# Two-bank PSUM tiles for the scores and the transposed probabilities of a windowed attention

## The chip, the cores and the metric

The kernel runs on one core of one Trainium2 chip. The metric is the device time of one execution in microseconds (us), taken as the median of several runs. The engines in this text are PE (TensorE, its weight loads are listed as PEld), DVE (VectorE), ACT (ScalarE), POOL (GpSimd) and SP, which issues DMAs. PSUM, the memory that PE writes its results to, is used here in eight banks, each of 512 float32 values on 128 partitions.

## The reference, cut to what matters

One decoder layer with two branches is computed for a prompt of 2048 positions and for a small group of 64 sampled positions. The change touches only the first branch, a grouped-query attention with a window of 128 positions, 8 query heads, 2 key/value heads and 64 values per head:

```python
d = qpos - kpos
band = (d >= 0) & (d <= WINDOW)                       # 128 queries against 256 keys
s = jnp.einsum('...qhgd,...khd->...hgqk', q, k).astype(jnp.float32) * (ATT_HEAD_DIM ** -0.5)
s = jnp.where(mask, s, NEG)
p = jax.nn.softmax(jnp.concatenate([s, sink], axis=-1), axis=-1)[..., :-1]
return jnp.einsum('...hgqk,...khd->...qhgd', p.astype(v.dtype), v)
```

The second branch (a gated linear attention) and the output projection follow it in the program and are the same before and after.

## The kernel before

`phase_a1` takes the first 400 us of the program, then `phase_gla` and `phase_out` follow. It works on 16 tiles of 128 prompt positions and one tile of 64 sampled ones. Each tile passes through the stages that `pipeline` (L537) staggers: `load`, `front` (norm of the input, with a broadcast of the row factors through a PSUM tile `pt` at L224), `dense` (the projection to q, k, v, 48 matmuls `pd` at L302 per tile), `rope`, `a` (`attna`, the scores and the softmax) and `b` (`attnb`, the product with the values). The first three tiles in `k.order1` are `early`: their `front` and `dense` are written ahead of the pipeline. The order of the instructions on each engine is made by the framework's scheduler from the program order, the priorities in `pipeline` and the buffers that are free. So a change of buffers moves instructions.

In `attna` the queries and keys are transposed on PE into `pq` (L387) and `pk` (L391). The scores of a tile come in two groups `g` of four heads. For each of two `j`, three products (L410: high times high, high times low, low times high) are written for `u` = 0 and `u` = 1 in turn. `u` is the key/value head: the product contracts over 64 rows, and `u` = 0 uses the lower 64 rows of the PE array, `u` = 1 the upper 64. Each `u` has its own PSUM tile `sc`. DVE then reads each head's 128x256 scores with the mask added (L415), which also gives the row maximum.

In `attnb` the probabilities are transposed on PE (L432) in blocks `pp` of four heads, two blocks per block of 128 keys. DVE copies the block of heads 0 to 3 (L433), which belong to `kv` = 0, and ACT that of heads 4 to 7, which belong to `kv` = 1. The value product `po` (L437) has one matmul for each `kv`, and they use the left 64 and the right 64 columns of the PE array.

The eight PSUM banks before are: two for `pd` (L302), three for `sc`, `pq` and `pk` in turn (pool `ps_s`), one for `po`, and two for `pp`, the broadcast `pt` and small uses at the start and in `gate` (pool `ps_t`). The projections of the second and third tile borrow banks of `ps_s` and `ps_o` (L294).

Of the kernel before, what the change touches and what calls it, by code (L numbers as in the profile page):

```python
# [95 lines left out]
def c_rows(k, sp, pp, w, name):  # L96

    nc = k.nc
    n = int(np.prod(w[0].shape[1:]))
    ps = pp.tile([P, 512], F32, tag="pt", name=name)  # L100
    for d in range(NC):
        r = slice(d % 4 * 32, d % 4 * 32 + 32)
        nc.tensor.matmul(ps[r, :n], k.cT[:, d, :], w[d], start=(d < 4), stop=(d >= 4),
                         tile_position=(0, r.start), skip_group_check=True)
    m = sp.tile([P, 512], F32, tag="crows", name="s" + name, bufs=2)
    nc.vector.tensor_copy(m[:, :n], ps[:, :n])
    return m


def modulation(k, cp, sp, pp, after):  # L110
# [14 lines left out]
    for j in range(NC + 1):  # L125
        if j < NC:
            m[j] = c_rows(k, sp, pp, [w[j][:, d] for d in range(NC)], f"mod{j}")
        if j > 0:
            d = j - 1
            ps = pp.tile([P, 2, 9], F32, tag="pt", name=f"modT{d}")  # L130
# [18 lines left out]
def phase_a1(k, cp, dp):  # L149
# [5 lines left out]
    with ExitStack() as es:  # L155
# [27 lines left out]
        with tc.tile_pool(name="a1m", bufs=1) as mp:  # L183
            for d, w in modulation(k, cp, mp, ps_t, lambda j: [load(early[n]) for n, m in ((0, 0), (1, 0), (2, 1)) if m == j]):
                nc.scalar.copy(whi[:, d, :], w)
                nc.vector.tensor_tensor(wlo[:, d, :], w, f(whi[:, d, :]), op=ALU.subtract)
# [16 lines left out]
        def front(i):  # L203
# [13 lines left out]
            else:  # L217
# [5 lines left out]
                pt = ps_t.tile([P, 1, 512], F32, tag="pt", name=f"pt{i}")  # L223
                nc.tensor.matmul(pt[:, 0, :T], k.ones[:T], diag[:T, :T], start=True, stop=True)  # L224
                nc.vector.tensor_tensor(h[:, :, :T], h[:, :, :T], pt[:, :, :T].to_broadcast((P, NC, T)), op=ALU.mult)
# [60 lines left out]
        def dense(i):  # L286
# [7 lines left out]
            banks = [(ps_s, "sc"), (ps_s if n == 1 else ps_o, "sc" if n == 1 else "po")] if n in (1, 2) else [(ps_d, "pd")] * 2  # L294
            pd = [pool.tile([P, 512], F32, tag=tag, name=f"pd{i}_{lo}") for (pool, tag), (lo, _) in zip(banks, rg)]
# [85 lines left out]
        def attna(i):  # L381
# [3 lines left out]
            pq = ps_s.tile([P, 4, P], F32, tag="sc", name=f"pq{i}")  # L385
# [4 lines left out]
            pk = ps_s.tile([P, 4, P], F32, tag="sc", name=f"pk{i}")  # L390
# [13 lines left out]
            for g in range(2):  # L404
                scs = [ps_s.tile([P, 2, 2 * P], F32, tag="sc", name=f"sc{i}_{g}_{u}") for u in range(2)]
                for j in range(2):
                    for n, (qa, ka) in enumerate(((0, kThi), (0, kTlo), (1, kThi))):
                        for u in range(2):
                            b = u * 64
                            nc.tensor.matmul(scs[u][:, j, :w], qT[b:b + 64, qa, 2 * g + j, :],  # L410
                                             ka[b:b + 64, sl, :], start=(n == 0), stop=(n == 2))
                for u in range(2):
                    for j in range(2):
                        h = 4 * u + 2 * g + j
                        nc.vector.tensor_tensor_reduce(  # L415
                            out=sm[:, h, :w], in0=scs[u][:, j, :w], in1=mk.rearrange("p a b -> p (a b)"), scale=1.0,
# [4 lines left out]
        def attnb(i):  # L421
# [23 lines left out]
        def attn_sample():  # L445
# [7 lines left out]
            pq = ps_t.tile([P, 4, P], F32, tag="pt", name="spq")  # L453
# [16 lines left out]
            for g in range(2):  # L470
                pt = ps_t.tile([P, 4, P], F32, tag="pt", name=f"spk{g}")
# [3 lines left out]
            pt = ps_t.tile([P, 4, P], F32, tag="pt", name="spkn")  # L475
# [4 lines left out]
            for bg in range(2):  # L480
                for kv in range(2):
                    sc = ps_s.tile([P, 2, 2 * P], F32, tag="sc", name=f"ssc{bg}_{kv}")
# [13 lines left out]
            pt = ps_t.tile([P, 4, P], F32, tag="pt", name="spp0")  # L496
# [3 lines left out]
            pt = ps_t.tile([P, 4, P], F32, tag="pt", name="spp1")  # L500
# [29 lines left out]
        def gate(i):  # L530
            if i == k.order1[8]:
                gate_rows(k, sp, ps_t, dp)
# [523 lines left out]
def gate_rows(k, sp, pp, dp):  # L1056
# [5 lines left out]
    for n in range(2):  # L1062
# [8 lines left out]
        for c0, c1 in ((0, P), (P, 192)):  # L1071
            pg = pp.tile([P, 512], F32, tag="pt", name=f"gb{n}_{c0}")
# [151 lines left out]
```

## Time and profile before

| | us |
|---|---|
| median of 3 runs | 1648.79 |
| lowest and highest run | 1646.57 and 1651.33 |
| the profiled execution | 1654.62 |
| its span in the trace | 1652.8 |
| mean granted clock of PE, of 1 | 0.962 |
| PE busy in the span | 1558.2 (94%) |

The span is the time from the first to the last instruction that the trace holds. The profiled execution is 1.8 us longer than its span, and 5.8 us (0.35%) longer than the median of the runs. The granted clock is the share of full speed that PE's throttle gave: 1.00 is 2.4 GHz, 0.5 is 1.2 GHz, and a value between them is a mean over a stretch with both levels. `phase_a1` ends at about 396 us of the span. From 414 to 1240 us the gated linear attention runs, and from 1322 us the output projection.

### The profile page before, as it was taken

How to read it: one execution, taken by the hardware profiler on the slowest of the kernel's cores; microseconds unless marked ns; L12 is line 12 of the kernel's file. 1: busy time of each engine (PE TensorE's matmuls, PEld its weight loads, DVE VectorE, ACT ScalarE, POOL GpSimd, SP SyncE). 2: the span in 40 equal slices, each digit the busy share in tenths (PEclk: the TensorE clock that was granted, in tenths of full speed). 3: DMA queues.
4: the chain of work that ended last, by engine and by line, in shares of the span. 5: the costliest groups of instructions: out<-in, count | busy, mean ns of one | idle time of the engine just before them, and what ended most of it. 6: DMA issues, size and time to landing. Idle time of an engine off the chain costs nothing.

```text
span 1652.8 us, 27244 instructions
## 1 busy us (share of the span) xinstructions
PE 1558.2 (94%) x9528; PEld 1357.5 (82%) x9528; DVE 1089.5 (66%) x2232; ACT 710.8 (43%) x1665; POOL 476.2 (29%) x553
## 2 busy tenths in 40 slices
PE   7789999897999999999999999999996699999998
PEld 5676766564999999899999999988895588888996
DVE  5886868855676788555777767778771165646442
ACT  3677857644334344333444445454451132313120
POOL 1885784733535444210212121124110000000000
PEclk9989999977999999999999999999998799999999
DMA  9875482672665554988676689876878977867632
GB/s 372 261 221 157 141 265 70 183 309 82 222 198 195 177 179 163 331 289 267 199 215 206 186 287 347 263 239 190 280 238 323 369 261 237 277 221 208 215 118 83
DMA packets 313182, 373.80 MB, mean 226 GB/s; under 512 B 37890, under 2 KB 229267, under 8 KB 307669
## 3 DMA queue, kind: packets, MB, share of 16 engines
q1 hardware_dynamic: 313044, 372.07, 68.9%
q8 instruction: 75, 1.23, 0.3%
q14 instruction: 63, 0.51, 0.1%
HBM read 248.91 MB, written 123.08 MB: 225 GB/s over the span
## 4 chain that ended last, share of the span: by engine, by line
PE 74%; DMA 9%; DVE 8%; ACT 3%; POOL 2%; issue 2%; SPq 2%; DVEq 0%; ACTq 0%; POOLq 0%
PE e L1045 10%; PE a L928 10%; PE d L928 10%; PE c L928 9%; PE q L583 9%; PE pd L302 6%; PE b L928 5%; PE g_l L784 3%; PE po L437 2%; PE sc L410 2%; PE pp L432 2%; DMA wo<-sw_e 1%; DMA s<-zm 1%; DMA o<-wo 1%; DVE tot L702 1%
## 5 line engine op out<-in xcount | busy, mean ns | idle before, releaser
L609 DVE TENSOR_TENSOR w<-r,w 128x512 fp32r<-128x512 f32 x272 | 203.5, 757 | 98.1 <-ACT w L608 88.0
L608 ACT CAST w<-r 128x512 fp32r<-128x512 f32 x272 | 165.8, 620 | 156.5 <-PE d L928 40.5
L928 PE MATMUL d<-x,w 128*128 128x384 f32 (+1 forms) x1152 | 206.7, 326 | 5.8 <-DVE u L937 2.3
L928 PE MATMUL c<-x,w 128*128 128x384 f32 (+1 forms) x1152 | 207.8, 326 | 3.4 <-ACT u L935 2.5
L928 PE MATMUL a<-x,w 128*128 128x384 f32 (+1 forms) x1152 | 209.4, 328 | 0.7 <-ACT w L608 0.7
L583 PE MATMUL q<-d_o,u_b 128*128 128x512 f32 (+1 forms) x960 | 189.7, 358 | 12.9 <-DMA d_o<-o 9.5
L928 PEld LDWEIGHTS d<-x,w 128*128 128x128 f32 x1152 | 189.0, 190 | 8.6 <-DVE u L937 2.8
L583 PEld LDWEIGHTS q<-d_o,u_b 128*128 128x128 f32 x960 | 162.3, 192 | 39.0 <-issue 13.0
L1045 PE MATMUL e<-wo,d_m 128*128 128x512 f32 x768 | 179.2, 394 | 13.9 <-DMA wo<-sw_e 13.9
L928 PEld LDWEIGHTS c<-x,w 128*128 128x128 f32 x1152 | 186.9, 189 | 5.7 <-ACT u L935 2.7
L928 PEld LDWEIGHTS a<-x,w 128*128 128x128 f32 x1152 | 188.4, 191 | 3.3 <-ACT w L608 1.0
L1045 PEld LDWEIGHTS e<-wo,d_m 128*128 128x128 f32 x768 | 146.0, 191 | 45.1 <-issue 14.7
L302 PE MATMUL pd<-whi,hs 128*128 128x512 f32 (+1 forms) x512 | 143.5, 362 | 7.1 <-DVE hs L240 4.4
L938 POOL TENSOR_TENSOR oc<-u,u 128x384 f32<-128x384 f32 (+1 forms) x48 | 69.4, 1445 | 273.5 <-DVE u L937 131.7
L302 PEld LDWEIGHTS pd<-whi,hs 128*128 128x128 f32 x512 | 92.4, 196 | 26.5 <-DVE hs L240 4.6
L928 PE MATMUL b<-x,w 128*128 128x384 f32 (+1 forms) x576 | 110.4, 332 | 0.5 <-ACT w L608 0.5
L928 PEld LDWEIGHTS b<-x,w 128*128 128x128 f32 x576 | 96.9, 193 | 2.1 <-ACT w L608 1.0
L302 PE MATMUL pd<-wlo,hs 128*128 128x512 f32 (+1 forms) x256 | 91.8, 361 | 0.0
L1011 ACT ACTIVATE s<-s 128x512 f32<-128x512 f32 (+1 forms) x64 | 41.1, 645 | 108.5 <-DMA s<-zm 106.6
L373 ACT ACTIVATE sm<-sm,nm,rs 128x256 f32<-128x256 f32 (+1 forms) x128 | 74.5, 587 | 7.8 <-DVE nm L369 7.4
L1023 DVE TENSOR_TENSOR s<-q,s 128x512 f32<-128x512 f32 (+1 forms) x40 | 23.1, 596 | 78.5 <-PE q L583 42.9
L736 DVE TENSOR_TENSOR KQ<-KQ,M 128x512 f32<-128x512 f32 (+2 forms) x115 | 71.9, 626 | 0.0
(249 smaller groups left out, 2638.7 us busy)
## 6 DMA issues: line engine op xcount, KB each, us to landing
r<-in_w_x SPq DMA_DIRECT2D x160, 256.0 KB
r<-tw SPq DMA_DIRECT2D x128, 256.0 KB
u_b<-sw_b SPq DMA_DIRECT2D x16, 2048.0 KB
x<-xd SPq DMA_DIRECT2D x14, 1536.0 KB
zm<-oc SPq DMA_DIRECT2D x48, 384.0 KB
xd<-sx SPq DMA_DIRECT2D x32, 512.0 KB
tw<-t SPq DMA_DIRECT2D x64, 256.0 KB
s<-zm SPq DMA_DIRECT2D x64, 256.0 KB
```

Source lines behind the costliest of these rows:

```text
L302: nc.tensor.matmul(pd[u][:T, :hi - lo], hs[:, d // 4, a, d % 4, :T], (whi, wlo)[b][:, d, lo:hi], start=(d == 0 and n == 0), stop=(d == NC ...
L373: nc.scalar.activation(sm[:, h, :w], sm[:, h, :w], AF.Exp, scale=0.125 if rq is None else rs[:, h:h + 1], bias=nm[:, h:h + 1], accum_out=d ...
L410: nc.tensor.matmul(scs[u][:, j, :w], qT[b:b + 64, qa, 2 * g + j, :], ka[b:b + 64, sl, :], start=(n == 0), stop=(n == 2))
L583: nc.tensor.matmul(ps[u][:, :s1 - s0], w[a][:, r, cs:cs + P], x[xr[n0]][:, b, s0:s1], start=(n0 == 0 and n == 0), stop=(n0 == len(rows) - ...
L608: nc.scalar.copy(w[:, 0], src)
L609: nc.vector.tensor_tensor(w[:, 1], src, f(w[:, 0]), op=ALU.subtract)
L736: nc.vector.tensor_tensor(out.rearrange("p a (n m) -> p a n m", m=m), x.rearrange("p a (n m) -> p a n m", m=m), M[r, b, at[n]:at[n + 1]].u ...
L784: nc.tensor.matmul(pl[:T, r, j, l - l0, :H], KQ[rr, l, j] if l else c["kT"][rr, j, :T], KQ[rr, l, 2 + j].rearrange("p (n s m) -> p n s m", ...
L928: nc.tensor.matmul(bank[b], wt[:, x, d], X[p][:, y, d], start=(p > 3 or p == 0) and d == 0 and n == 0, stop=(d == 3 and n == 2), skip_grou ...
L938: nc.gpsimd.tensor_tensor(oc[1][:, 1], t[2], t[1], op=ALU.add)
L1011: nc.scalar.activation(t[:, :N], t[:, :N], AF.Sigmoid)
L1045: nc.tensor.matmul(ps, mp[:, a, r, o0:o0 + T], wo[:, b, r, cs], start=(r == 0 and n == 0), stop=(r == 7 and n == 2))
```

## The change

The pools `ps_s` and `ps_t` are cut up in another way, with the same eight banks in all.

- `ps_s` now holds one tile of two banks. `scs[:, u]` is the bank of one `u`, so one tile holds a whole group of scores, for both `u`.
- `ps_t` now holds one tile `pq` of one bank (`one`) and one tile `pp` of two banks (`two`). `pq` serves the broadcast `pt`, the transposed queries `pq` and keys `pk` (which were in `ps_s`) and small uses. `pp` serves the transposed probabilities of all eight heads of a block of keys.
- The copies of `pp` are divided otherwise: DVE takes the first two heads of each bank (heads 0, 1, 4, 5) and ACT the last two of each (2, 3, 6, 7). Before, each took one bank.
- The projection of the second tile uses the two banks of `sc`, that of the third tile the bank of `pq` and the one of `po`.

No arithmetic is added or taken away.

```diff
-        ps_s = es.enter_context(tc.tile_pool(name="a1ps", bufs=3, space=PSUM))
+        ps_s = es.enter_context(tc.tile_pool(name="a1ps", bufs=1, space=PSUM))
...
-        ps_t = es.enter_context(tc.tile_pool(name="a1pt", bufs=2, space=PSUM))
+        ps_t = es.enter_context(tc.tile_pool(name="a1pt", bufs=1, space=PSUM))
+        one = lambda name: ps_t.tile([P, 512], F32, tag="pq", name=name)
+
+        two = lambda name: ps_t.tile([P, 2, 512], F32, tag="pp", name=name)
+        heads = lambda ap: ap.rearrange("p (h t) -> p h t", h=4)
...
-                pt = ps_t.tile([P, 1, 512], F32, tag="pt", name=f"pt{i}")
-                nc.tensor.matmul(pt[:, 0, :T], k.ones[:T], diag[:T, :T], start=True, stop=True)
+                pt = one(f"pt{i}")[:, :T]
+                nc.tensor.matmul(pt, k.ones[:T], diag[:T, :T], start=True, stop=True)
...
-            banks = [(ps_s, "sc"), (ps_s if n == 1 else ps_o, "sc" if n == 1 else "po")] if n in (1, 2) else [(ps_d, "pd")] * 2
-            pd = [pool.tile([P, 512], F32, tag=tag, name=f"pd{i}_{lo}") for (pool, tag), (lo, _) in zip(banks, rg)]
+            if n == 1:
+                pd = ps_s.tile([P, 2, 512], F32, tag="sc", name=f"pd{i}")
+                pd = [pd[:, u] for u in range(2)]
+            elif n == 2:
+                pd = [one(f"pd{i}_0"), ps_o.tile([P, 512], F32, tag="po", name=f"pd{i}_512")]
+            else:
+                pd = [ps_d.tile([P, 512], F32, tag="pd", name=f"pd{i}_{lo}") for lo, _ in rg]
...
-            pq = ps_s.tile([P, 4, P], F32, tag="sc", name=f"pq{i}")
+            pq = heads(one(f"pq{i}"))
...
-            pk = ps_s.tile([P, 4, P], F32, tag="sc", name=f"pk{i}")
+            pk = heads(one(f"pk{i}"))
...
-                scs = [ps_s.tile([P, 2, 2 * P], F32, tag="sc", name=f"sc{i}_{g}_{u}") for u in range(2)]
+                scs = ps_s.tile([P, 2, 2, 2 * P], F32, tag="sc", name=f"sc{i}_{g}")
...
-                for g in range(2):
-                    pt = ps_t.tile([P, 4, P], F32, tag="pt", name=f"pp{i}_{n}_{g}")
-                    for j in range(4):
-                        nc.tensor.transpose(pt[:, j, :], sm[:, g * 4 + j, n * P:(n + 1) * P], k.ident)
-                    (nc.scalar.copy if g else nc.vector.tensor_copy)(pT[:, n, g * 4:g * 4 + 4, :], pt)
+                pt = two(f"pp{i}_{n}").rearrange("p g (j t) -> p g j t", j=4)
+                for h in range(8):
+                    nc.tensor.transpose(pt[:, h // 4, h % 4, :], sm[:, h, n * P:(n + 1) * P], k.ident)
+
+                for u in range(2):
+                    (nc.scalar.copy if u else nc.vector.tensor_copy)(
+                        pT[:, n].rearrange("p (g j) t -> p g j t", g=2)[:, :, 2 * u:2 * u + 2], pt[:, :, 2 * u:2 * u + 2])
```

The rows below are instructions in the order in which one engine runs them: the line of the code, the operation, output and inputs by their names in the program (the first number in a name is the tile), the size of what moves, and the semaphores it waits on by engine. On PE, the second group of scores of tile 6 before (`sc6_1_0` is `u` = 0, `sc6_1_1` is `u` = 1, whose last five matmuls follow):

```order
L410 MATMUL sc6_1_0_2167<-kThi_338,qT6_2140 128x256
L410 MATMUL sc6_1_0_2167<-kTlo_339,qT6_2140 128x256
L410 MATMUL sc6_1_0_2167<-kThi_338,qT6_2140 128x256 x2
L410 MATMUL sc6_1_0_2167<-kTlo_339,qT6_2140 128x256
L432 MATMUL pp4_1_0_2062<-ident_137,sm4_1684 128x128 [waits DVE_49]
L432 MATMUL pp4_1_0_2062<-ident_137,sm4_1684 128x128 x3
L410 MATMUL sc6_1_0_2167<-kThi_338,qT6_2140 128x256
L302 MATMUL pd8_0_1996<-wlo_104,hs8_1663 128x512
L302 MATMUL pd8_0_1996<-whi_103,hs8_1663 128x512 x2
L302 MATMUL pd8_0_1996<-wlo_104,hs8_1663 128x512
L302 MATMUL pd8_0_1996<-whi_103,hs8_1663 128x512
L410 MATMUL sc6_1_1_2168<-kThi_338,qT6_2140 128x256 [waits DVE_49]
```

The same group on PE after, all twelve matmuls, behind the projection of tile 10:

```order
L311 MATMUL pd10_512_2432<-whi_103,hs10_2104 128x272 x2
L311 MATMUL pd10_512_2432<-wlo_104,hs10_2104 128x272
L311 MATMUL pd10_512_2432<-whi_103,hs10_2104 128x272
L419 MATMUL sc6_1_2144<-kThi_338,qT6_2118 128x256 [waits DVE_49]
L419 MATMUL sc6_1_2144<-kThi_338,qT6_2118 128x256
L419 MATMUL sc6_1_2144<-kTlo_339,qT6_2118 128x256 x2
L419 MATMUL sc6_1_2144<-kThi_338,qT6_2118 128x256 x4
L419 MATMUL sc6_1_2144<-kTlo_339,qT6_2118 128x256 x2
L419 MATMUL sc6_1_2144<-kThi_338,qT6_2118 128x256 x2
```

The six matmuls of `u` = 0 ran one after another before, ahead of the six of `u` = 1; now the two alternate. On PE, the four value matmuls of tile 4 before (`v3` and `v4` are the values of its two key blocks, with one matmul per `kv` each):

```order
L437 MATMUL po4_2048<-pT4_2049,v3_1164 64x512 [waits Activation_49]
L432 MATMUL pp4_1_1_2068<-ident_137,sm4_1684 128x128 [waits DVE_49]
L432 MATMUL pp4_1_1_2068<-ident_137,sm4_1684 128x128 x3
...
L437 MATMUL po4_2048<-pT4_2049,v3_1164 64x512 [waits Activation_49]
L437 MATMUL po4_2048<-pT4_2049,v4_1382 64x512
...
L437 MATMUL po4_2048<-pT4_2049,v4_1382 64x512 [waits Activation_49]
```

On PE, the transposes and the value product of tile 5 after:

```order
L440 MATMUL pp5_1_2255<-ident_137,sm5_1911 128x128 [waits Activation_49]
L440 MATMUL pp5_1_2255<-ident_137,sm5_1911 128x128 x7
L448 MATMUL po5_2242<-pT5_2243,v4_1372 64x512 x2
L396 MATMUL pq7_2354<-ident_137,rq_7_2082 128x128 [waits DVE_49]
L396 MATMUL pq7_2354<-ident_137,rq_7_2082 128x128 x3
L311 MATMUL pd11_0_2700<-whi_103,hs11_2318 128x512 [waits DVE_49]
L311 MATMUL pd11_0_2700<-wlo_104,hs11_2318 128x512
L311 MATMUL pd11_512_2701<-whi_103,hs11_2318 128x272 [waits Activation_49]
L311 MATMUL pd11_512_2701<-wlo_104,hs11_2318 128x272
L448 MATMUL po5_2242<-pT5_2243,v5_1613 64x512 [waits Activation_49]
L448 MATMUL po5_2242<-pT5_2243,v5_1613 64x512
```

Before, three separate places held the four matmuls of a tile; now two places hold two each. On ACT, the copies of tile 6's probabilities before, with the rows around the second:

```order
L433 COPY pT6_2512<-pp6_0_1_2519 128x512 [waits PE_49,Activation_49]
...
L331 COPY lr_60<-raw10_2458 128x16
L433 COPY pT6_2512<-pp6_1_1_2531 128x512 [waits PE_49]
L278 CAST sx6_11_2364<-s6_11_2362 128x512 [waits DMAHW6_49,DVE_49]
L278 CAST sx2_11_2370<-s2_11_2368 128x512 [waits DMAHW7_49,DVE_49]
```

And on ACT after:

```order
L443 COPY pT6_2484<-pp6_0_2485 128x2x256 [waits DVE_49]
L232 ACTIVATE h12_2349<-h12_2349,B_70,A_69 128x128 [waits DVE_49]
L232 ACTIVATE h12_2349<-h12_2349,B_70,A_69 128x128 x7
L443 COPY pT6_2484<-pp6_1_2496 128x2x256 [waits DVE_49]
L382 ACTIVATE sm7_2366,dn7_2404<-sm7_2366,nm7_2402,rs87_2406 128x256 [waits DVE_49,Pool_49]
```

ACT's copy waited for PE's transposes before; now it waits for DVE, whose own copy of the same two banks goes first.

## Rows read from the trace of the kernel before

**Rows 1.** The page: span and busiest engines, with share of the span.

```profile
span 1652.8 us, 27244 instructions
PE 1558.2 (94%) x9528; PEld 1357.5 (82%) x9528; DVE 1089.5 (66%) x2232; ACT 710.8 (43%) x1665; POOL 476.2 (29%) x553
```

**Rows 2.** Stretches of the span: each engine's busy us (instructions), clock, DMA.

```profile
core 0: us, PE busy (x) PEld busy (x) DVE busy (x) ACT busy (x) POOL busy (x), PEclk, DMA share, GB/s
46.00:130.00 84.00, 70.48 (x373) 58.20 (x372) 72.11 (x183) 60.82 (x164) 71.28 (x94) 0.84 0.81 249
130.00:315.00 185.00, 177.60 (x972) 118.30 (x970) 148.16 (x389) 123.88 (x344) 120.16 (x169) 1.00 0.54 159
315.00:396.00 81.00, 74.52 (x387) 46.87 (x385) 45.83 (x140) 41.79 (x123) 31.29 (x48) 0.83 0.56 205
414.00:1240.00 826.00, 810.20 (x5711) 780.36 (x5711) 601.20 (x1123) 363.50 (x821) 235.82 (x215) 0.99 0.73 234
```

**Rows 3.** The chain of waits of 130 to 315 us, by line.

```profile
by line: PE pd L302 36.0%; PE po L437 12.5%; PE sc L410 10.8%; PE pp L432 8.3%; DVE mx L365 3.4%; DVE sm L378 2.9%; DMA sgate<-in_b_gate 2.7%; DVE sm L415 2.2%; PE pq L387 2.2%; PE gb L1073 2.1%; PE gate L103 2.1%; DVE s L276 2.1%; issue 1.
```

**Rows 4.** Timeline of PE, scores: start us, us, line and operation, count.

```profile
252.14 0.39 PE L410 MATMUL sc<-kThi,qT 64*128 64x256 f32 x2
252.37 0.28 PE L410 MATMUL sc<-kTlo,qT 64*128 64x256 f32 x1
252.49 0.28 PE L410 MATMUL sc<-kThi,qT 64*128 64x256 f32 x1
252.70 0.66 PE L387 MATMUL pq<-ident,rq 128*128 128x128 f32 x4
...
256.61 0.40 PE L410 MATMUL sc<-kThi,qT 64*128 64x256 f32 x4
256.84 0.29 PE L410 MATMUL sc<-kTlo,qT 64*128 64x256 f32 x2
```

**Rows 5.** Timeline of PE, value product; each L437 matmul is two records.

```profile
380.90 1.08 PE L437 MATMUL po<-pT,v 128*64 128x512 f32 x4
381.91 0.66 PE L432 MATMUL pp<-ident,sm 128*128 128x128 f32 x4
...
382.60 1.07 PE L437 MATMUL po<-pT,v 128*64 128x512 f32 x2
383.61 0.66 PE L432 MATMUL pp<-ident,sm 128*128 128x128 f32 x4
```

**Rows 6.** Stretch 130 to 315 us, L410 alone, then L437 alone.

```profile
130.00:315.00 185.00, 27.82 (x216) 21.49 (x216) 1.00 0.54 159
130.00:315.00 185.00, 36.58 (x80) 6.63 (x80) 1.00 0.54 159
```

**Rows 7.** Groups by line: busy us, mean ns of one, idle before.

```profile
L415 DVE CUSTOM_DVE_ANT_0 sm<-sc,band 128x256 f32<-128x256 f32 (+1 forms) x128 | 46.3, 409 | 19.0 <-PE sc L410 16.4 <-PE gate L103 2.6
L415 DVE DVE_READ_ACCUMULATOR2_ANT mx<- 128x1 f32 x128 | 10.3, 81 | 0.0
L433 DVE COPY pT<-pp 128x512 f32<-128x512 f32 x31 | 21.3, 686 | 19.2 <-PE pp L432 9.8 <-issue 5.2 <-PE po L437 4.0
L433 ACT COPY pT<-pp 128x512 f32<-128x512 f32 x31 | 18.0, 581 | 17.7 <-PE pp L432 17.7
```

**Rows 8.** Timelines of 50 to 76 us: the start of tiles 3 and 4.

```profile
50.07 0.38 PE L224 MATMUL pt<-diag,ones 128*128 128x128 f32 x2
...
64.85 2.39 POOL L247 TENSOR_TENSOR hs<-h,hs 128x1024 fp32r<-128x1024 f32 x1
...
68.57 0.47 PE L302 MATMUL pd<-whi,hs 128*128 128x512 f32 x1
...
71.27 1.21 DVE L225 TENSOR_TENSOR h<-h,pt 128x1024 f32<-128x1024 f32 x1
...
72.51 3.19 ACT L228 ACTIVATE h<-h,B,A 128x128 f32<-128x128 f32 x8 [1.75 <-DVE h L225]
```

**Rows 9.** Timeline of PE at the phase's end, idle us and releaser in brackets.

```profile
385.90 0.65 PE L432 MATMUL pp<-ident,sm 128*128 128x128 f32 x4 [0.79 <-DVE pT L433]
387.80 1.93 PE L437 MATMUL po<-pT,v 128*64 128x512 f32 x6 [1.25 <-ACT oT L440]
...
399.89 0.73 PE L682 MATMUL g_z<-lrT,wg 17*128 17x128 f32 x4 [3.68 <-DMA wg<-in_w_gate]
```

More of the change, by code (lines that the diff above doesn't have):

```diff
@@ L99, in c_rows @@
     n = int(np.prod(w[0].shape[1:]))
-    ps = pp.tile([P, 512], F32, tag="pt", name=name)
+    ps = pp[1](name)[:, 0]
     for d in range(NC):
@@ L129, in modulation @@
             d = j - 1
-            ps = pp.tile([P, 2, 9], F32, tag="pt", name=f"modT{d}")
+            ps = pp[0](f"modT{d}")[:, :18].rearrange("p (u n) -> p u n", u=2)
             for u in range(2):
@@ L183, in phase_a1 @@
         with tc.tile_pool(name="a1m", bufs=1) as mp:
-            for d, w in modulation(k, cp, mp, ps_t, lambda j: [load(early[n]) for n, m in ((0, 0), (1, 0), (2, 1)) if m == j]):
+            for d, w in modulation(k, cp, mp, (one, two), lambda j: [load(early[n]) for n, m in ((0, 0), (1, 0), (2, 1)) if m == j]):
                 nc.scalar.copy(whi[:, d, :], w)
@@ L222, in front @@
                 nc.gpsimd.tensor_scalar(diag[:T, :T], k.ident[:T, :T], rs[:T, 0:1], 1.0, op0=ALU.mult, op1=ALU.mult)
[L223 to L225 removed]
+                pt = one(f"pt{i}")[:, :T]
+                nc.tensor.matmul(pt, k.ones[:T], diag[:T, :T], start=True, stop=True)
+                nc.vector.tensor_tensor(h[:, :, :T], h[:, :, :T], pt.unsqueeze(1).to_broadcast((P, NC, T)), op=ALU.mult)
                 if i < NPT:
@@ L409, in attna @@
                             b = u * 64
-                            nc.tensor.matmul(scs[u][:, j, :w], qT[b:b + 64, qa, 2 * g + j, :],
+                            nc.tensor.matmul(scs[:, u, j, :w], qT[b:b + 64, qa, 2 * g + j, :],
                                              ka[b:b + 64, sl, :], start=(n == 0), stop=(n == 2))
@@ L415, in attna @@
                         nc.vector.tensor_tensor_reduce(
-                            out=sm[:, h, :w], in0=scs[u][:, j, :w], in1=mk.rearrange("p a b -> p (a b)"), scale=1.0,
+                            out=sm[:, h, :w], in0=scs[:, u, j, :w], in1=mk.rearrange("p a b -> p (a b)"), scale=1.0,
                             scalar=-3e38, op0=ALU.add, op1=ALU.max, accum_out=mx[:, h:h + 1])
@@ L452, in attn_sample @@
                 nc.sync.dma_start(O["sv"][b, 120:128], v[b * 8:b * 8 + 8, :])
-            pq = ps_t.tile([P, 4, P], F32, tag="pt", name="spq")
+            pq = heads(one("spq"))
             for g in range(4):
@@ L470, in attn_sample @@
             for g in range(2):
-                pt = ps_t.tile([P, 4, P], F32, tag="pt", name=f"spk{g}")
+                pt = heads(two(f"spk{g}")[:, 0])
                 for j in range(4):
@@ L474, in attn_sample @@
                 nc.scalar.copy(kT[:, g * 4:g * 4 + 4, 0:P], pt)
-            pt = ps_t.tile([P, 4, P], F32, tag="pt", name="spkn")
+            pt = heads(one("spkn"))
             nc.tensor.transpose(pt[:, 0, :T], kk[:T].rearrange("p a d -> p (a d)"), k.ident[:T, :T])
@@ L480, in attn_sample @@
             for bg in range(2):
+                scs = ps_s.tile([P, 2, 2, 2 * P], F32, tag="sc", name=f"ssc{bg}")
                 for kv in range(2):
-                    sc = ps_s.tile([P, 2, 2 * P], F32, tag="sc", name=f"ssc{bg}_{kv}")
+                    sc = scs[:, kv]
                     for bl in range(4):
@@ L495, in attn_sample @@
             pT = sp.tile([P, 2, 4, P], F32, tag="pT", name="spT", bufs=1)
-            pt = ps_t.tile([P, 4, P], F32, tag="pt", name="spp0")
+            pt = heads(two("spp0")[:, 0])
             for n in range(4):
@@ L499, in attn_sample @@
             nc.scalar.copy(pT[:, 0], pt)
-            pt = ps_t.tile([P, 4, P], F32, tag="pt", name="spp1")
+            pt = heads(one("spp1"))
             for n in range(4):
@@ L531, in gate @@
             if i == k.order1[8]:
-                gate_rows(k, sp, ps_t, dp)
+                gate_rows(k, sp, (one, two), dp)
         for fn in (front, dense, combine):
@@ L1071, in gate_rows @@
         for c0, c1 in ((0, P), (P, 192)):
-            pg = pp.tile([P, 512], F32, tag="pt", name=f"gb{n}_{c0}")
+            pg = pp[0](f"gb{n}_{c0}")
             nc.tensor.matmul(pg[:c1 - c0], sel[:, c0:c1], m, start=True, stop=True)
```

## The prediction

> **What bounds the kernel now.** I read the page's totals first: PE is busy for 94% of the span [rows 1]. That is a mean over stages, so the second view is the table of stretches [rows 2]. The change lies in the first 396 us, and there one stretch is plainly PE's: from 130 to 315 us PE is busy for 177.6 of 185 us at full clock, with DVE behind it at 148.2. The chain of waits agrees: projection, value product, scores and transposes lead it, and no line of another engine has over 3.4% [rows 3]. From 46 to 130 us DVE, POOL and PE are all between 70 and 72 us of 84, a start in which each waits for the others. From 315 to 396 us PE is busy for 74.5 of 81 us, though at a mean clock of 0.83, and at its end the pieces of idle time before PE wait for DVE's copies and ACT's output copy [rows 9]. What follows hangs on the end of this phase: the branch behind it has PE busy for 810.2 of 826 us [rows 2], its order is left as it was, and so I let a shift of the phase's end pass through one to one.
>
> **What the change takes away: PE time.** The scores use half of the array's rows and the value product half of its columns. The timeline shows what a pair of halves costs. Four score matmuls of both halves take 0.23 us until the next one starts, 0.115 for a pair, and two of one half alone also take 0.23 us, 0.115 each [rows 4]. So the partner is free. A value product of two matmuls in one place takes 1.01 us until the next instruction, and a single one takes 1.01 us as well [rows 5].
>
> How many pairs there are is a count in the order of both programs. Scores: 93 of 192 possible pairs stood together before and 198 matmuls stood alone, 291 steps in all; now there are 192 pairs, 99 steps fewer. Value product: 11 pairs and 40 alone, 51 steps; now 31 pairs, 20 fewer. The reason is in the buffers. With one tile for both halves, the scheduler gets both halves free at once; and with each copy taking half of both banks, the two value matmuls of a key block become ready together. The array is also switched less between whole, half rows and half columns: 168 times in place of 228. A score step ahead of a switch takes 0.21 us in place of 0.12 [rows 4], so 0.09 for each.
>
> The sum over the phase is 99 x 0.115 = 11.4 us, 20 x 1.01 = 20.2 and 60 x 0.09 = 5.4: 37 us of PE's time. The stretch from 130 to 315 us holds 216 of 384 scores and 80 of the 124 records of the value product [rows 6], so 6.4 + 13.0 + 3.2 (0.59 of the switches, an estimate from the same shares) = **22.6 us**. The rest splits into some 10 us behind it and 4 us ahead of it.
>
> For these switches the Trainium skill has a rule (TensorEngine Tiling (Array Packing), Key Properties): a change of the tiling mode drains TensorE. The 0.09 us in the row agrees; by a drain that overlapped with other work, 5.4 us of the sum would be 0.
>
> **What it adds: waits for single buffers.** Scores had three banks in turn, now a group must be read before the next can be written. Four reads by DVE of 0.409 + 0.081 us [rows 7] are 1.96 us between the last score of group 0 and the first of group 1. The same holds for the transposes: the second key block waits for both copies. DVE took 0.686 and ACT 0.581 us [rows 7] side by side on their own banks; now ACT's waits on DVE's, 1.27 us in a row. Behind these waits on PE stand the scores or transposes and then everything that PE has queued, the projection above all; behind ACT's wait stand the eight activations of a later tile. Fully exposed this is 16 x 1.96 + 15 x 1.27 = 50.4 us, and at no cost at all it is 0.
>
> The order after says what PE has between. I added up, with durations of the trace, the work of PE between group 0 and group 1 of each tile, 0 to 15: 4.9, 3.0, 2.2, 1.9, 3.3, 1.7, 3.2, 0.3, 0.1, 1.9, 1.9, 2.1, 4.1, 0.4, 0.4, 1.8 us, mostly projection. Taken from 1.96 this leaves 3.9 us open in the long stretch, from tiles 7 and 8 nearly alone, and 3.2 in tiles 13 to 15. For the transposes of tiles 1 to 15 the cover is 2.4, 0.7, 3.2, 1.9, 3.2, 0.8, 0.2, 0.7, 2.5, 2.2, 2.7, 2.6, 0.7, 0, 0, which leaves 2.7 open in the long stretch and 3.1 in the last tiles. To the 6.6 us of the long stretch I add an estimate of 4 us for DVE's queue: a read or a copy that became ready can stand behind one long operation, such as the multiply of 1.21 us [rows 8], and DVE is busy for 0.8 of the stretch; three or four such hits in nine tiles. Its ends are 0 and 9 x 1.21 = 11 us.
>
> On the copies the Trainium skill speaks against the change (PSUM — Partial Sum Buffer, PSUM bank collisions raise a hardware error): two engines may not touch one bank in the same partitions at once, reads included, so they must be put in a row. The rows of before only show copies of different banks. Without that rule the two copies would take 0.69 us in place of 1.27, and the 2.7 us above would be below 1.
>
> **The start.** The third tile's projection now sits in the one bank that the broadcast `pt` of tile 3 needs too. In the order after, that broadcast is behind the whole projection of tile 2; before, it ran at 50.07 us and tile 3's projection began at 68.57 [rows 8]. After, the chain can begin only there: 0.38 for the broadcast, 1.21 on DVE, 3.19 on ACT, 2.39 on POOL [rows 8], so tile 3 starts at 75.8 us at the earliest, 7.2 later. Against this stand 4 us of PE saved here, other work of PE that moves into the gap, and a POOL queue which from tile 6 on has less ahead of the next tile's input than before. Dense work runs three tiles ahead of the scores and can give a delay back. I take **0** for this stretch, with ends of -4 and +10.
>
> **The end.** In the last 81 us PE saves 10 us, loses 6.3 to the open waits, and sits in a chain with DVE, ACT and POOL, where the rows already show idle time ahead of transposes [rows 9]. What PE saves there becomes longer idle time. I take **0**, with ends of -6 and +6.
>
> **The sum.** -22.6 + 6.6 + 4 + 0 + 0 = **-12 us**. Against the profiled execution of 1654.6 us that is 1642.6; it was 5.8 us above the median, so against the median of 1648.8 I predict **1637 us**. The ends of the open terms give 1629 to 1643 for this case.
>
> **The rivals.**
>
> (1) *Nearly all is realised.* The stretch keeps its 22.6 less 6.6, the end gives 10 - 3 and the start 4, with nothing lost to DVE's queue: about -28, so 1620 us (1612 to 1629). DVE's 148.2 us in the long stretch would still fit under its new 160. Against it: the end and the start are not PE's alone.
>
> (2) *The start is paid in full.* Tile 3 comes 7.2 us late, and one more POOL operation of 2.39 in front, since POOL is busy for 71.3 of 84 us there [rows 2]: 9.6 us that later tiles don't give back. -12 + 9.6 = -2.4, so 1646 us, no change that can be told. For it: the start is a chain in which each tile waits for the one before. Against it: the long stretch has PE work ready to fill with.
>
> (3) *Slower: the single score tile and the serial copies take PE's place as the bound.* If DVE doesn't reach its reads while PE has cover, three quarters of the 50.4 us open up, and half of 16 x 1.21 us of DVE's queue on top: 37.8 + 9.7 = 47.5 us against the 37 saved, +11, so 1660 us. The point from which it decides is 37 of 70 us, half of what could be exposed. For it: DVE is at 0.8 of the stretch, the scheduler's order fixes the cover by modelled times, and the reads have other operations between them on DVE. Against it: by the order, 10 of 16 tiles have the full cover.
>
> (4) *The change doesn't do what it says*: the pairs stand together in the order, yet don't run together. Then only 3.2 us of switches are saved in the long stretch against 10.6 of waits, +7, so 1656 us. [rows 4, 5] speak against it: pairs ran together before.
>
> **How the numbers follow.** A measurement of this kernel can tell a change from none from about 0.3% on, 5 us: faster is below 1643.8, slower above 1653.7. The chances are 0.48 for the forecast, 0.18 for (1), 0.17 for (2), 0.14 for (3) and 0.03 for (4). Faster is 0.48 + 0.18 = 0.66, the same 0.17, slower 0.14 + 0.03 = 0.17. The range of 8 in 10 takes the forecast, (2), the upper two thirds of (1) and the edge of (3) and (4): 1617 to 1655 us.
>
> **What would show it.** In the timeline of the changed kernel, scores should come in 12 matmuls of some 1.4 us without gaps and value products as two matmuls of 1.0 us; PE's busy time from the scores and the value product should fall by some 30 us over the phase. The idle time of PE ahead of scores, put down to DVE's reads, should be some 4 to 8 us in the long stretch, and that ahead of transposes, put down to ACT's copies, 3 to 5. Tile 3's projection should start near 76 us. I am wrong if the phase ends later than 392 us of the span, or if the idle time of PE ahead of scores and transposes sums to more than 25 us.

## The result, and the profile after

The changed kernel takes 1701.2 us (median; 1699.1 to 1701.9) against 1648.2 for the kernel before: a ratio of 1.032, with a 95% interval of 1.030 to 1.034. The ratio goes by the means of the runs; by it the kernel is 52 us slower, where 12 us faster was forecast. Of the two profiled executions that of before lay 5.8 us above its median and that of after 2.1 us below, so the traces show 44 of the 52 us. The page of the changed kernel, span and busy times of the engines, against [rows 1]:

```profile
span 1697.2 us, 27224 instructions
PE 1539.0 (91%) x9528; PEld 1348.7 (79%) x9528; DVE 1087.0 (64%) x2232; ACT 713.7 (42%) x1665; POOL 476.0 (28%) x553
```

The span grew by 44.4 us while PE's busy time fell by 19. All of that lies in the attention phase. Its last value product ends at 443.4 us (before: 396.2), 47.2 us later, and the rest of the program takes 1253.8 us in place of 1256.6. So the stretch from 46 us to the phase's end is the one to compare. Of the kernel before (columns as in [rows 2]):

```profile
46.00:396.20 350.20, 322.80 (x1728) 223.37 (x1726) 266.10 (x710) 226.49 (x629) 222.73 (x310) 0.92 0.61 191
```

And of the changed kernel:

```profile
46.00:443.40 397.40, 307.71 (x1720) 217.31 (x1718) 266.45 (x702) 227.69 (x627) 220.37 (x310) 0.85 0.53 168
```

PE is busy for 15.1 us less and idle for 62.3 us more (27.4 before, 89.7 after). Its mean granted clock fell from 0.92 to 0.85. DVE, ACT and POOL do the same work as before in a longer stretch: none of them became a bound. What became of the pairs is seen in the groups (line, operation, count, busy us and mean ns, idle time ahead and what ended it), of the kernel before:

```profile
L302 PE MATMUL pd<-whi,hs 128*128 128x512 f32 (+1 forms) x512 | 143.5, 362 | 7.1 <-DVE hs L240 4.4 <-POOL hs L247 1.0 <-DVE raw L67 0.9
L437 PE MATMUL po<-pT,v 128*64 128x512 f32 x124 | 57.2, 640 | 1.4 <-ACT oT L440 1.2
```

And of the changed kernel:

```profile
L311 PE MATMUL pd<-whi,hs 128*128 128x272 f32 (+1 forms) x512 | 150.6, 377 | 23.0 <-POOL hs L251 10.8 <-DVE hs L250 6.7 <-ACT raw L314 2.6
L448 PE MATMUL po<-pT,v 128*64 128x512 f32 x124 | 40.3, 729 | 14.4 <-ACT pT L443 14.2
L419 PE MATMUL sc<-kThi,qT 64*128 64x256 f32 (+1 forms) x256 | 36.5, 337 | 9.9 <-DVE mx L424 9.2 <-ACT kThi L365 0.7
L419 PE MATMUL sc<-kTlo,qT 64*128 64x256 f32 (+1 forms) x128 | 21.5, 329 | 5.7 <-DVE kTlo L366 5.7
L440 PE MATMUL pp<-ident,sm 128*128 128x128 f32 x248 | 42.4, 309 | 10.3 <-ACT pT L443 7.7 <-POOL sm L387 2.1 <-ACT spT L511 0.3
```

All the scores together (PE busy, PEld busy, clock, DMA), before and after:

```profile
46.00:396.20 350.20, 54.08 (x384) 42.80 (x384) 0.92 0.61 191
46.00:443.40 397.40, 39.29 (x384) 30.01 (x384) 0.85 0.53 168
```

The value product is busy for 40.3 us where it was 57.2, and the scores for 39.3 where they were 54.1: 31.7 us less. PE's whole busy time fell by only 15.1, since the rest of its work took longer: the projection, the same matmuls, has a mean of 377 ns where it had 362, with the mean clock at 0.85 in place of 0.92. The waits of PE before, from 46 us to the phase's end (who waited for whom: us in total, times, longest):

```profile
PE pd L302 <- DVE hs L240: 4.4, 1, 4.4
PE pp L432 <- DVE mx L368: 3.6, 1, 3.6
...
PE pp L432 <- DVE pT L433: 1.2, 3, 0.8
...
PE sc L410 <- DVE mx L415: 0.4, 1, 0.4
```

And after:

```profile
PE po L448 <- ACT pT L443: 14.2, 9, 3.0
PE pd L311 <- POOL hs L251: 10.8, 8, 4.8
PE sc L419 <- DVE mx L424: 9.2, 8, 2.6
PE pp L440 <- ACT pT L443: 7.7, 7, 2.2
PE pd L311 <- DVE hs L250: 6.7, 4, 2.4
PE pk L400 <- DVE qT L366: 5.8, 3, 2.5
PE sc L419 <- DVE kTlo L366: 5.7, 2, 5.3
```

Waits for reads and copies of single tiles (`mx`, `pT`) went from 1.6 to 31.1 us, those for copies of queries and keys out of their bank (`qT`, `kTlo`) from 2.7 to 11.5, and those for the projection's input (`hs`, all lines) from 5.4 to 21.4.

### The profile page after: what moved, and what is told of

Its sections match the earlier page's. It is cut to its first block, busy times and chain, and to the rows that moved or that the text cites. A ratio compares the mean times of both kernels' runs of the same rounds, so it can differ in the third digit from the quotient of the medians.

```text
span 1697.2 us, 27224 instructions
## 1 busy us (share of the span) xinstructions
PE 1539.0 (91%) x9528; PEld 1348.7 (79%) x9528; DVE 1087.0 (64%) x2232; ACT 713.7 (42%) x1665; POOL 476.0 (28%) x553
## 4 chain that ended last, share of the span: by engine, by line
PE 66%; DVE 11%; DMA 10%; ACT 4%; POOL 4%; issue 3%; SPq 2%; DVEq 0%; POOLq 0%; ACTq 0%
PE e L1057 10%; PE a L940 9%; PE d L940 9%; PE c L940 9%; PE q L595 8%; PE pd L311 5%; PE b L940 5%; PE g_l L796 3%; DVE sm L424 1%; DMA s<-zm 1%; ACT sm L382 1%; DMA wo<-sw_e 1%; DVE sm L387 1%; DMA xd<-sx 1%; PE pp L440 1%
## 5 line engine op out<-in xcount | busy, mean ns | idle before, releaser
L621 DVE TENSOR_TENSOR w<-r,w 128x512 fp32r<-128x512 f32 x272 | 203.7, 758 | 97.4 <-ACT w L620 92.0
L311 PE MATMUL pd<-whi,hs 128*128 128x272 f32 (+1 forms) x512 | 150.6, 377 | 23.0 <-POOL hs L251 10.8
L311 PEld LDWEIGHTS pd<-whi,hs 128*128 128x128 f32 x512 | 97.7, 206 | 53.3 <-POOL hs L251 14.4
```

What stands on the lines that cost most here:

```text
L311: nc.tensor.matmul(pd[u][:T, :hi - lo], hs[:, d // 4, a, d % 4, :T], (whi, wlo)[b][:, d, lo:hi], start=(d == 0 and n == 0), stop=(d == NC ...
L621: nc.vector.tensor_tensor(w[:, 1], src, f(w[:, 0]), op=ALU.subtract)
```

## The experiments

Each ratio is against the kernel before on the same chip; a difference in us between two experiments is that of their ratios, times 1648. The first theory, A, came from the order. In the changed kernel the transposes of a tile stand next to the scores of the next tile; before, they stood next to the scores of the tile after that. The rows ahead of the prediction show `pp4` beside `sc6` before; after, the transposes of tile 5 run from 222.5 to 228.9 us and the scores of tile 6 from 222.2 to 227.9. Between 14 pairs of neighbours, the scores of the next tile were complete ahead of the transposes in 12 cases before and in 2 after. The softmax of some 16 us would then no longer be hidden. Theory B was that the tiles that exist only once cost it, with the two copies in a row. Some expectations name two more: C, that PE's saved time is real and the loss comes from tiles that exist only once; and D, that PE's time does not count.

**e1, pt away from the bank of pq and pk, into the tile of transposes**

```diff
-                pt = one(f"pt{i}")[:, :T]
+                pt = two(f"pt{i}")[:, 0, :T]
```

> The changed kernel with one line changed back in effect: the broadcast pt of the norm is written to the two-bank tile pp and no longer to the one bank that pq and pk use. Paired scores, two-bank transposes and divided copies all stay. Theory A (the one bank is handed out in program order to pt of tile t+4, pq of tile t and pk of tile t, so that the scores of the next tile come behind the transposes of this one on PE, and the softmax of some 16 us is no longer hidden): the scores of the next tile stand ahead of the transposes again, and most of the 52 us come back: 1630 to 1655 us. Theory B (the single score tile and the two copies in a row cost it): nothing of that is touched, 1690 to 1702 us.

Measured: 1697.6 us, 1.033 (1.030 to 1.035). The order was mended and the time was not, so the order alone isn't the cause, and theory A in that form fell. But `pt` had only moved from one tile that exists once to another.

**e2, the kernel before with pt, pq and pk in one bank**

```diff
-        ps_s = es.enter_context(tc.tile_pool(name="a1ps", bufs=3, space=PSUM))
+        ps_s = es.enter_context(tc.tile_pool(name="a1ps", bufs=2, space=PSUM))
+        ps_q = es.enter_context(tc.tile_pool(name="a1pq", bufs=1, space=PSUM))
+        one = lambda name: ps_q.tile([P, 512], F32, tag="pq", name=name)
...
-                pt = ps_t.tile([P, 1, 512], F32, tag="pt", name=f"pt{i}")
+                pt = one(f"pt{i}")[:, :T]
...
-            pq = ps_s.tile([P, 4, P], F32, tag="sc", name=f"pq{i}")
+            pq = heads(one(f"pq{i}"))
...
-            pk = ps_s.tile([P, 4, P], F32, tag="sc", name=f"pk{i}")
+            pk = heads(one(f"pk{i}"))
```

> The kernel before with only pt, pq and pk put into one bank, two banks left for the scores, which stay unpaired, and the transposes and copies as before. Theory A: this alone gives the loss, 1680 to 1710 us, with some 20 us from one tile's scores to the next. Theory B: no single score tile, no copies in a row, so about as before, 1645 to 1660 us.

Measured: 1685.4 us, 1.026 (1.023 to 1.028). It has no tile of two banks, and most of the loss is there.

**e7, the same with pt back among the transposes**

```diff
-                pt = one(f"pt{i}")[:, :T]
+                pt = ps_t.tile([P, 1, 512], F32, tag="pt", name=f"pt{i}")
```

> As the run with pt, pq and pk in one bank and unpaired scores (1685 us), but with pt back among the transposes: only pq and pk share the one bank, and the scores have two. The scores of the next tile are ahead of the transposes in 12 of 14 tiles, as before. If it is the sharing of pq and pk that costs (there, PE was idle for 15.1 us ahead of pk on the copies of pq), about 1670 to 1685 us; if it is pt between them, 1643 to 1655 us.

Measured: 1646.9 us, 1.000 (0.998 to 1.002). So `pq` and `pk` may share a bank, and the scores do not need the third bank; `pt` between them costs 2.6%, 43 us. The timelines of PE show how. First e2 (start us, us, line and operation), the broadcast of tile 9, `pq` and `pk` of tile 5 and the first scores of tile 5:

```profile
181.62 0.39 PE L227 MATMUL pt<-diag,ones 128*128 128x128 f32 x2
...
185.97 0.66 PE L394 MATMUL pq<-ident,rq 128*128 128x128 f32 x4
...
191.19 0.27 PE L398 MATMUL pk<-ident,rk 128*128 128x128 f32 x1
...
198.24 0.39 PE L417 MATMUL sc<-kThi,qT 64*128 64x256 f32 x2
```

In e7, `pq` of tile 5, then the broadcast of tile 8, `pk` and the first scores of tile 5, `pq` of tile 6, and only then the broadcast of tile 9:

```profile
149.24 0.66 PE L394 MATMUL pq<-ident,rq 128*128 128x128 f32 x4
...
158.71 0.49 PE L227 MATMUL pt<-diag,ones 128*128 128x128 f32 x2
159.54 0.28 PE L398 MATMUL pk<-ident,rk 128*128 128x128 f32 x1
...
164.74 0.38 PE L417 MATMUL sc<-kThi,qT 64*128 64x256 f32 x2
...
168.52 0.66 PE L394 MATMUL pq<-ident,rq 128*128 128x128 f32 x4
...
172.07 0.49 PE L227 MATMUL pt<-diag,ones 128*128 128x128 f32 x2
```

The pipeline writes the norm of tile 9 ahead of the scores of tile 5, and a bank that exists once is handed out in that order. In e2 the scores of tile 5 therefore stand behind a norm four tiles ahead, and start at 198.2 us; in e7 they pass it and start at 164.7. The changed kernel has the same chain, with its scores of tile 5 at 203.7 us:

```profile
183.29 0.39 PE L228 MATMUL pt<-diag,ones 128*128 128x128 f32 x2
...
189.07 0.66 PE L396 MATMUL pq<-ident,rq 128*128 128x128 f32 x4
...
194.79 0.30 PE L400 MATMUL pk<-ident,rk 128*128 128x128 f32 x1 [2.54 <-DVE qT L366]
203.72 0.38 PE L419 MATMUL sc<-kThi,qT 64*128 64x256 f32 x2
```

**e8 and e9, the changed kernel with pt and pk, and with pt alone, in the projection's banks**

```diff
-                pt = one(f"pt{i}")[:, :T]
+                pt = ps_d.tile([P, 512], F32, tag="pd", name=f"pt{i}")[:, :T]
```

```diff
-            pk = heads(one(f"pk{i}"))
+            pk = heads(ps_d.tile([P, 512], F32, tag="pd", name=f"pk{i}"))
```

(e9 is the first edit alone, e8 both.)

> The changed kernel with pt and pk written to the two banks of the projection, so that the one bank holds pq alone. Scores of the next tile come ahead of the transposes in 13 of 14 tiles. Theory A: 1645 to 1660 us. Theory C: the waits for the copies and the reads stay, and only the 11 us ahead of pk and of the products with the low part of the keys go: 1680 to 1692 us.

> The changed kernel with only the broadcast pt written to the two banks of the projection; pq and pk share the one bank, and the two-bank tiles stay. If pt is the cause of the larger part (handed out in program order, pt of tile t+4 must come ahead of pq of tile t, so scores wait for a norm four tiles ahead), about as with pt and pk moved (1667): 1660 to 1675 us, and the scores of tile 5 no longer start behind the broadcast of tile 9. If pk behind pq in one bank was the cause, 1690 to 1702 us.

Measured: 1667.0 us, 1.013 (1.008 to 1.017), which lies between the two ranges of e8, and 1669.3 us, 1.013 (1.009 to 1.016). The one line on `pt` takes 32 of the 52 us away, and `pk` adds nothing to it. Twenty remain.

**e3 and e4, the kernel before with only the score tile, and only the tile of transposes**

```diff
-        ps_s = es.enter_context(tc.tile_pool(name="a1ps", bufs=3, space=PSUM))
+        ps_s = es.enter_context(tc.tile_pool(name="a1ps", bufs=1, space=PSUM))
...
-                scs = [ps_s.tile([P, 2, 2 * P], F32, tag="sc", name=f"sc{i}_{g}_{u}") for u in range(2)]
+                scs = ps_s.tile([P, 2, 2, 2 * P], F32, tag="sc", name=f"sc{i}_{g}")
```

(e3, with `pq` and `pk` in their own bank as in e7.)

```diff
-                    pt = ps_t.tile([P, 4, P], F32, tag="pt", name=f"pp{i}_{n}_{g}")
...
+                pt = two(f"pp{i}_{n}").rearrange("p g (j t) -> p g j t", j=4)
```

(e4, with the divided copies; `pt`, `pq` and `pk` in the three banks of the scores.)

> The kernel before with only the two-bank score tile: pq and pk in a bank of their own, pt still with the transposes, transposes and copies as before. Theory A: scores of the next tile stay ahead of the transposes in 11 of 14 tiles, so no loss; the pairs save some 11 us of PE's time, 1635 to 1650 us. Theory B: 16 waits of 1.96 us on the reads open up, 1665 to 1680 us.

> The kernel before with only the two-bank transposes and the divided copies; the three banks of the scores also hold pt, pq and pk. Theory A: the scores of the next tile are ahead of the transposes in 9 of 14 tiles, so a part of the loss, 1650 to 1675 us. Theory B: 15 waits of 1.27 us and no pairs of scores gained, 1655 to 1668 us; the two are told apart by where PE is idle, ahead of transposes by B, ahead of the projection and the scores by A.

Measured: 1662.5 us, 1.012 (1.010 to 1.014), and 1679.2 us, 1.020 (1.018 to 1.022). e3 lies between its two ranges and e4 above both. Against e7, which differs from e3 by the score tile alone, that tile costs 1.2%, with all its pairs. In e4 a tile of transposes and a new place for `pt` are mixed, so it settles nothing.

**e6 and e16, the copies side by side**

```diff
+                for g in range(2):
+                    for j in range(4):
+                        nc.tensor.transpose(pt[:, g, j, :], sm[:, j // 2 * 4 + 2 * g + j % 2, n * P:(n + 1) * P], k.ident)
+                for g in range(2):
+                    (nc.scalar.copy if g else nc.vector.tensor_copy)(
+                        pT[:, n].rearrange("p (v j) t -> p v j t", v=2)[:, :, 2 * g:2 * g + 2], pt[:, g].rearrange("p (v j) t -> p v j t", v=2))
```

(e6 in the changed kernel, e16 in e9; the lines shown stand in place of its transposes and copies of a key block. One two-bank tile still holds both banks.)

> The changed kernel, all its tiles and its 31 pairs as they are, but each copy takes one whole bank of the two-bank tile (DVE's bank holds heads 0, 1, 4, 5, ACT's holds 2, 3, 6, 7), so ACT's copy no longer waits for DVE's. Theory C: in the trace of the changed kernel PE is idle for 14.2 us ahead of value products and 7.7 us ahead of transposes on ACT's copy; 0.6 us off each of 31 copies gives back 10 to 20 us, 1680 to 1692 us. Theory A (the order, with the scores of the next tile behind the transposes of this one, sets the pace): the order is the same, 1695 to 1702 us.

> The changed kernel with pt in the projection's banks (1669 us), and each copy from one bank of the two-bank tile (mixed heads), so that ACT's copy need not wait for DVE's. With pt's tie gone, the 0.58 us of each key block may show: 1655 to 1665 us if the copies in a row matter, 1667 to 1673 us if not.

Measured: 1706.7 us, 1.036 (1.032 to 1.040), and 1673.9 us, 1.016 (1.012 to 1.020). Neither is faster, and both lie above their ranges, e6 by 5 us and e16 by 1. But the edits did not do what they were made for. The Trainium skill's rule on banks (PSUM — Partial Sum Buffer, PSUM bank collisions raise a hardware error) asks for the copies in a row where both engines read one bank. In e6 and e16 each copy has a bank of its own, and the row stayed all the same. ACT's copy starts after the end of DVE's in all 31 places of e6 and of e16, in 12 of those in e6 only 0.03 us after it. ACT's waits ahead of its copy, in the changed kernel, in e6, and in e14 (below), where the transposes have two single banks:

```profile
ACT pT L443 <- DVE pT L443: 23.3, 12, 4.4
...
ACT pT L443 <- DVE pT L443: 21.6, 12, 3.4
...
ACT pT L441 <- PE pp L440: 12.1, 12, 1.9
```

So the part of theory B that blamed the copies in a row was not tested. Why the row stayed, no run shows; that both banks are still one tile may be the reason.

**e5, the kernel before with the heads mixed, and e10, with pt in the projection's banks on top**

```diff
-                        nc.tensor.transpose(pt[:, j, :], sm[:, g * 4 + j, n * P:(n + 1) * P], k.ident)
-                    (nc.scalar.copy if g else nc.vector.tensor_copy)(pT[:, n, g * 4:g * 4 + 4, :], pt)
+                        nc.tensor.transpose(pt[:, j, :], sm[:, j // 2 * 4 + 2 * g + j % 2, n * P:(n + 1) * P], k.ident)
+                    (nc.scalar.copy if g else nc.vector.tensor_copy)(
+                        pT[:, n].rearrange("p (v j) t -> p v j t", v=2)[:, :, 2 * g:2 * g + 2], pt.rearrange("p (v j) t -> p v j t", v=2))
```

> The kernel before, all its banks as they were; only which heads go into which one-bank block of transposes is changed: heads 0, 1, 4, 5 into the block that DVE copies, 2, 3, 6, 7 into the one that ACT copies. So the value product stands in 31 pairs, as in the changed kernel, yet no tile of two banks exists and the two copies run side by side. Theory C (PE's saved time is real, and the loss comes from tiles that exist only once): 20 us of PE's time saved, 1625 to 1640 us. Theory D (PE's time does not count, since the phase waits for DVE, ACT and POOL): 1643 to 1650 us.

> The kernel before with the mixed heads (1634.6 us) and also pt in the banks of the projection. In that kernel the transposes of tile t come some 4 us behind the broadcast of tile t+5 in tiles 2 to 6, as the order of their shared two banks asks. If that tie costs time there too, 1615 to 1630 us; if the two banks of transposes are the better place, 1632 to 1650 us, with the projection's matmuls waiting for the norm's multiplication instead.

Measured: 1634.6 us, 0.992 (0.989 to 0.995), and 1633.0 us, 0.992 (0.989 to 0.995). e5 is the changed kernel's idea for the value product without its banks: two single banks, each copied whole, each with two heads of either half. It has 31 pairs and is 13 us faster than the kernel before. So PE's time does count here. Moving `pt` from where it was before adds nothing.

**e11 and e12, the mixed heads on e7, and the score tile on top of that**

The edit of e11 is that of e5, and e12 adds that of e3.

> The kernel with pq and pk in one bank and two banks for unpaired scores (1647 us), and the mixed heads on top. If the 20 us of PE's time of the value product count here as they did in the kernel before (13 to 14 us), 1630 to 1636 us; if the phase now waits for the chain of norm, softmax and copies, 1643 to 1650 us.

> The run above with one change: the two banks of the scores are one tile, so all 192 pairs of scores stand together. If the single score tile costs what the earlier two runs showed (1662 against 1647 us, 16 us), 1645 to 1655 us; if that was a matter of the order in one program, the 11 us of PE's time that the pairs save show: 1620 to 1635 us.

Measured: 1665.9 us, 1.011 (1.007 to 1.014), and 1668.8 us, 1.011 (1.007 to 1.015). Both lie above both of their ranges: the edit that gave 13 us to the kernel before took 18 from e7. e15 below is e11 with the line of `pt` moved and nothing else, and the loss becomes a gain of 13. So this loss, too, hangs on where `pt` is; why the same place costs nothing in e7 or e5, no run shows. On e11 the score tile costs nothing (e12), where on e7 it cost 1.2% (e3). A single run of such an edit proves little.

**e13, e14 and e15, a square with e9**

In all four `pt` is in the projection's banks, `pq` and `pk` share a bank, and the value product has 31 pairs. e13 has the scores in two tiles and the transposes in one of two banks, e14 the other way round, e15 no two-bank tile at all. The edits to e9 are those of e3 taken back (e13), and of e5 in place of the two-bank block (e14), and both (e15). In e14 and e15 the small uses are back in the banks of the transposes as well.

> The changed kernel with pt in the projection's banks (1669 us), and the two banks of the scores as two tiles again, unpaired; the two-bank transposes with divided copies stay. If the single score tile carries the remaining 20 us: 1645 to 1655 us. If the two-bank transposes or the bank of pq and pk do: 1665 to 1680 us.

> The changed kernel with pt in the projection's banks (1669 us), and the transposes in two single banks again, with the mixed heads so that the 31 pairs of value products stay; the single score tile stays. If the two-bank tile of transposes carries the remaining 20 us: 1640 to 1652 us. If the score tile or the bank of pq and pk do: 1662 to 1675 us.

> Both of the above: no two-bank tile is left, pt in the projection's banks, pq and pk in one bank, mixed heads. If the two-bank tiles carry the remaining 20 us, 1628 to 1640 us, near the mixed heads alone; if the bank of pq and pk does, 1655 to 1670 us.

Measured: 1682.0 us, 1.022 (1.018 to 1.025); 1669.1 us, 1.013 (1.009 to 1.018); 1634.7 us, 0.992 (0.990 to 0.995). e13 is 2 us above the higher of its ranges; the others lie within one of theirs. Without two-bank tiles the kernel is 13 us faster than before; with either of them, or both, 21 to 36 us slower. The prices do not add: put on e13, the score tile takes 15 us away (e9). The bank of `pq` and `pk` is cleared once more, with `pt` in this place. The stretch from 46 us to the phase's end in e9:

```profile
46.00:415.20 369.20, 296.05 (x1717) 209.54 (x1715) 262.73 (x701) 226.38 (x627) 227.14 (x310) 0.88 0.57 181
```

In e15:

```profile
46.00:376.50 330.50, 295.37 (x1713) 214.57 (x1711) 256.75 (x702) 224.68 (x626) 224.53 (x307) 0.91 0.63 202
```

And in e13, where the phase ends last of the four:

```profile
46.00:426.80 380.80, 313.31 (x1716) 226.41 (x1714) 268.82 (x703) 228.09 (x627) 227.10 (x311) 0.83 0.56 175
```

PE is busy alike in e9 and e15, 296 and 295 us, though e9 has the score pairs on top, at a clock of 0.88 against 0.91. Its idle time is 73 us against 35. The first waits of PE in e9:

```profile
PE sc L419 <- DVE mx L424: 13.5, 11, 2.7
PE pp L440 <- ACT pT L443: 13.4, 9, 4.3
PE po L448 <- ACT pT L443: 7.4, 5, 3.1
...
PE pd L311 <- DVE hs L245: 1.9, 2, 1.5
```

The same kinds in e15:

```profile
PE pp L439 <- DVE pT L440: 3.4, 5, 0.9
PE po L445 <- ACT pT L440: 3.1, 2, 1.8
...
PE sc L417 <- DVE mx L422: 2.3, 2, 1.2
```

That is 34.3 us of waiting for reads and copies against 8.8. The last line of e9 shows what went with the move of `pt`: the waits for the projection's input, 21.4 us in the changed kernel, are 1.9.

## Why the prediction was wrong

- **The pairs**: the mechanism was right, and nearly the size. A value product of two matmuls, four records, takes 1.01 us in the changed kernel as well, and 31 pairs are worth 13 us of the whole (e5). Scores and value product are busy for 31.7 us less, where some 30 were forecast. What the 37 us left out is that the rest of PE's work took longer, at a mean granted clock of 0.85 in place of 0.92: PE's whole busy time fell by 15.1 us. (The 1.4 us for twelve scores is twelve times 0.115, the price without pairs; six pairs take 0.90.)
- **The start**: this is the step that failed most. It saw that the broadcast `pt` shares a bank with the projection of the third tile, priced that for tile 3 alone, and took 0. For tile 3 the reading was good: all but the first four matmuls of its projection begin at 78.2 us, where about 76 was forecast. But the same bank also serves `pq` and `pk` of every tile. The tie "`pt` of tile t+4, then `pq` of tile t" holds all through the phase, and no term and no rival had it. It carries 32 of the 52 us (the changed kernel against e9), 43 in the kernel before (e2 against e7).
- **The waits for single buffers**: in the changed kernel the direct waits for reads ahead of scores were 9.2 us where 7.1 was left open, and those for copies ahead of transposes 7.7 where 5.8 was. With `pt` out of the way (e9) they are 13.5 and 13.4, so these terms were some half of what they cost. The sum also left out the value product's wait for ACT's copy, 14.2 us in the changed kernel and 7.4 in e9. Together, against e15, the two-bank tiles turn a gain of 13 us into a loss of 21 (e9). That is near rival (3), which had 1660 us; e9 has 1669. The nearness is partly luck, since it counted 47.5 us of such waits and of DVE's queue against 37 saved, and e9 shows 34.3 of such waits against some 27 of PE's busy time saved. Its point, half of the exposure, with 0.14 for it, was too kind. The cover was added up from matmuls that the order puts there, as if each were ready when its turn comes: in the changed kernel, 21.4 us of idle time for the projection's input say that it is not. The 4 us for DVE's queue were not measured apart.
- **ACT's copy behind DVE's**: priced by the rows at 2.7 us in the long stretch. No run takes the row away and leaves the tile, so its price stays open.
- **The end**: taken as 0, since saved time would turn into idle time. No run sets the last tiles apart. The program behind the phase gave little back: it takes 1256.6 us before, 1253.8 in the changed kernel, and 1248 to 1265 in the experiments.
- **The forecast's own tests** both spoke against it: it was to be wrong if the phase ended later than 392 us, and it ended at 443.4; or if PE's idle time ahead of scores and transposes was over 25 us, and it was 25.9 (9.9, 5.7 and 10.3). Rival (1) adds up to -27 us, not -28, which changes nothing.

What stays open is how the loss of the two-bank tiles divides into waits, the copies in a row, the clock and the scheduler's order. e14 and e13 against e15 say that either tile alone is enough there, and e12 against e11 that the score tile is free in another layout.

## What to carry to other kernels

A buffer that exists once is handed out in program order, so before two uses share one, write down which tile of each comes first. If the uses belong to stages that run several tiles apart, the sharing ties the stages together for the whole loop and not for the first tile alone. When two results must be ready together, try to change what goes into the buffers that are there (e5: the heads of each block) before merging the buffers: here the same pairs came at a gain of 13 us that way, and at a loss with merged ones. Even that edit must be measured where it will stand: on e7 it lost 18 us until `pt` was moved (e15). A cover for a wait counts only if the work in it is ready by then.

## What the runs showed of the hardware

The scores of both halves of the array ran at the price of one: in the changed kernel the twelve matmuls of a group, six pairs, take 0.90 us from the first to the next instruction. The mean granted clock of the phase was 0.92 and 0.91 where PE was busy for 0.92 and 0.89 of it (before, e15), and 0.85 and 0.83 where it was busy for 0.77 and 0.82 (after, e13); all four are means over the two levels, 2.4 and 1.2 GHz. The busy share alone does not set it: e2, busy for 0.83 of its phase, had 0.89.

```profile
46.00:434.90 388.90, 323.57 (x1729) 221.92 (x1727) 271.65 (x710) 227.63 (x629) 220.67 (x311) 0.89 0.55 172
```

A small operation of DVE can take as long as a large one of POOL beside it, but not beside every one. In the changed kernel the negated maximum of a tile (L378, 128x8) takes 0.17 us while POOL is in a power of 128x10 for 1.97 us, and 2.32 us in the next tile, while POOL is in a 2.73 us subtraction (start us, us, engine, line):

```profile
169.32 0.17 DVE L378 TENSOR_SCALAR nm<-mx 128x8 f32<-128x8 f32 x1
...
168.76 1.97 POOL L145 TENSOR_TENSOR rq<-rq,mhalf 128x10 f32<-128x10 f32 x1
...
191.65 2.32 DVE L378 TENSOR_SCALAR nm<-mx 128x8 f32<-128x8 f32 x1
...
191.21 2.73 POOL L251 TENSOR_TENSOR hs<-h,hs 128x1024 fp32r<-128x1024 f32 x1 [5.67 <-DVE hs L250]
```

The Trainium skill has a rule for it (SBUF — State Buffer, SBUF: two separate sides): the pair of ports that DVE shares with POOL is a lock, held for a whole instruction, for the DVE operations that use the pair. The long pair of rows agrees. The short pair does not: there the whole DVE operation lies inside POOL's. No run here tried it.
